# Moved in a two-layer trunk: 1/rms sums, a gate projection, filler products and stores

## The chip, the cores and the metric

The kernel runs on one core of a Trainium2 chip. The metric is the device time of one execution in microseconds (us), a median over runs. Engines: PE is TensorE, DVE is VectorE, ACT is ScalarE, POOL is GpSimd, SP is SyncE, which only issues DMAs here. PEclk is the granted clock of TensorE as a share of its full speed.

## The reference

One step of a streaming encoder trunk with two layers, on 1,024 new frames of one stream and 64 frames of another, 1,088 columns together, D_MODEL 1024, in float32. Each layer does `x += mixer(rmsnorm(x))` and then `x += sqrelu_mlp(rmsnorm(x))`; a last rmsnorm follows. Layer 0's mixer is sliding-window attention, layer 1's is a gated linear recurrence (HGRN2):

```python
def hgrn2_mix(h, s0, w_in, lb, out_norm, w_o):
    zq, zf, zi, zg = jnp.split(h @ w_in, ...)          # 8 heads of 128 each
    q = silu(zq); k = (1 - lb) * sigmoid(-zf); v = zi
    logf = jnp.log(lb + (1 - lb) * sigmoid(zf))
    o, S = hgrn_scan(q, k, v, logf, s0)                # chunks of 64 frames
    o = rmsnorm(o, out_norm) * silu(zg)
    return o.reshape(B, T, D) @ w_o, S

def sqrelu_mlp(h, w_up, w_down):                       # 1024 -> 4096 -> 1024
    return jnp.square(jax.nn.relu(h @ w_up)) @ w_down
```

## The kernel before

Activations lie with features on the partitions and the 1,088 columns along the free dimension: eight tiles of 128 features, two of them to a `pair` tile. Every product of float32 values is done as three matmuls of operands that are split in a high and a low part (high by high, high by low, low by high: lines 117, 118 and 119, in `up` lines 862 and 875). The high part is a cast on ScalarE, the low part a subtraction or a fused multiply and subtract on VectorE (line 108 for weights, 777 and 958 for activations).

The stages follow each other: attention (to about 353 us of the profiled execution), the MLP of layer 0 (to about 1134), the recurrence (to about 1740), the MLP of layer 1 (to the end). An MLP has three parts:

- `mix_rest` finishes the mixer's output projection. Output tiles d below `na` got the products of the first six input tiles already in the mixer's stage, from `mix_out`, where they serve as filler (NA = 6 tiles in attention, NB = 4 in the recurrence); `mix_rest` adds the last two input tiles for these and all eight for the others, then adds each product to x on VectorE (`mix_acc`, line 444), squares x on ScalarE and sums the squares over tiles on VectorE (`square_part`, line 157). Tiles 6 and 7 come last, in four column chunks of 272 (`CH4`). On the way it prepares the operands of `up`: b11, b12, t2, t4 and t3 for each of the four pairs of tiles.
- `up` multiplies with w_up by a Strassen-like scheme on halves of rows and columns (TH = 544 columns). The first two tiles are done plainly, by `whole(t, ps, i)`, 48 matmuls each: `whole(0, ps, 0)` needs b11 and b12, `whole(0, ps, 1)` needs b21 and b22, which `op.odd(p)` prepares. `norm(j)` multiplies the sums of squares of column half j with a matrix of ones on TensorE (line 845) and makes 1/rms from it on ScalarE and VectorE; `finish` (lines 881 to 883) applies it, squares, and stores the tile to y_mlp in HBM.
- `down` multiplies with w_down in five groups of 4, 8, 6, 8 and 6 input tiles. `hidden` loads an input tile from y_mlp (line 956, in GpSimd's DMA queue), and splits it (lines 957 and 958). x itself is parked in HBM (x_mlp) during `up` and reloaded at the start of `down`.

The recurrence makes, for each of eight heads, four projections of 72 matmuls (`proj`: f, q, v and the gate g), in three column chunks; `mix` does the scan with masked scores (its products stand at lines 601 to 696), and `tail` multiplies scores and states with v and q, normalises (lines 724 to 742) and applies the gate. The first projection goes ahead of its 1/rms: the raw product is ready in a bank of PSUM, `norm_scale` makes the sum over partitions in another (line 181) and 1/rms from it (lines 169 to 175), and VectorE multiplies (line 542). The pool `mm` has three banks there, the pool `psB` four.

The order in which each engine does its instructions isn't the written one: a planner orders them when the program is built, from estimated readiness, with the written order as priority. DMA issues are ordered in the same way in each engine's queue, and each queue is worked off in order.

Of the kernel before, what the change touches and what calls it, by code (L numbers as in the profile page):

```python
# [17 lines left out]
P = 128  # L18
# [9 lines left out]
TH = T // 2  # L28
# [5 lines left out]
EPS = 1e-5  # L34
NLEV = 5
NA = 6
NB = 4


class Trunk:  # L40
# [79 lines left out]
        return ps[:, :n], s, n  # L120


    def scaled(self, c):
        if c in self.due:
            self.due.remove(c)
            self.norm_scale(c)


    def banks(self, ctx, name, n):
# [2 lines left out]
    def bank(self):  # L132
        return self.mm.tile([P, 512], F32, name="mm", tag="mm")
# [40 lines left out]
        nc.vector.tensor_scalar(y[:, :n], y[:, :n], -0.5, 1.5, ALU.mult, ALU.add)  # L174
        nc.vector.tensor_mul(out, out, y[:, :n])

    def norm_scale(self, c):
        nc = self.nc
        s, n = self.CH[c]
        ps = self.bank()  # L180
        nc.tensor.matmul(ps[:, :n], self.ones[:], self.ss[:, s:s + n], start=True, stop=True)
        self.inv_root(self.rstd[:, s:s + n], ps[:, :n], n, D)

# [263 lines left out]
    def mix_rest(self, wa, wb, op, na):  # L447
        self.new_norm()
        ins = self.xin()

        def squares(k):
            for c in range(len(self.CH)):
                self.square_part(k, c)

        self.CH = CH64
        for d in range(6):
            if d >= na:
                w = self.weight(wa[d])
            elif d % 4 == 0:
                w = self.weight(wb[:, 2 * d:min(2 * na, 2 * d + 8), :], min(8, 2 * (na - d)))  # L460
            for c in range(3):
                if d < na:
                    self.mix_acc(w[2 * (d % 4):2 * (d % 4) + 2], ins[6:], d, c)
                else:
                    self.mix_acc(w, ins, d, c)
            squares(d)
            if d % 2:
                op.b11(d // 2)
                op.t24(d // 2)
        ws = [self.weight(wa[d]) for d in (6, 7)]  # L470
        self.CH = CH4
        for c in range(4):
            for d in (6, 7):
                self.mix_acc(ws[d - 6], ins, d, c)
        for p in range(3):
            op.b12(p)
        for p in range(3):
            op.t3(p)
        op.b11(3)
        op.b12(3)  # L480
        for d in (6, 7):
            squares(d)


    def recurrence(self):
        nc, tc, A, O = self.nc, self.tc, self.A, self.O
        with ExitStack() as ctx:
# [43 lines left out]
            def proj(piece):  # L531
                w = self.weight(A["w_in"][piece])
                z = hp.tile([P, T], F32, name="z", tag="z", bufs=3)
                ready = []
                for c in range(3):
                    if c == len(ready):
                        ready.append(self.product(w, self.xin(), c))
                    if c < 2 and c in self.due:
                        ready.append(self.product(w, self.xin(), c + 1))
                    ps, s, n = ready[c]  # L540
                    self.scaled(c)
                    nc.vector.tensor_mul(z[:, s:s + n], ps, self.rstd[:, s:s + n])
                return z

# [3 lines left out]
            def gates(h):  # L548
                r = {}
                z = proj(8 + h)  # L550
                r["f"] = f = hp.tile([P, T], F32, name="f", tag="f")
                bk = self.pair(3) if h % 2 else hp.tile([P, 2, T], F32, name="bk", tag="bk")
                r["b"], r["kk"] = b, kk = bk[:, 0, :], bk[:, 1, :]
                o_, l_ = om[:, h:h + 1], lb[:, h:h + 1]
                sig(f[:], z[:], 1.0)
                nc.vector.tensor_scalar(f[:], f[:], o_, l_, ALU.mult, ALU.add)
                t = tmp()
                nc.scalar.activation(t[:], f[:], AF.Ln)
                nc.vector.tensor_tensor_scan(b, reset[:], t[:], 0.0, ALU.mult, ALU.add)
                sig(kk, z[:], -1.0)  # L560
                nc.vector.tensor_scalar(kk, kk, o_, None, ALU.mult)

                z = proj(h)
                r["q"] = q = hp.tile([P, 9, 192], F32, name="q", tag="q", bufs=2)
                t = tmp()
                sig(t[:], z[:], 1.0)
                nc.vector.tensor_mul(q[:, :8, :P], z[:, :TP].rearrange("p (n t) -> p n t", t=P),
                                     t[:, :TP].rearrange("p (n t) -> p n t", t=P))
                nc.vector.tensor_mul(q[:, 8, :64], z[:, TP:], t[:, TP:])
                nc.vector.tensor_mul(q[:, :8, P:], q[:, :8, 1:P:2],  # L570
                                     f[:, :TP].rearrange("p (n t) -> p n t", t=P)[:, :, 1::2])
                nc.vector.tensor_mul(q[:, 8, 64:96], q[:, 8, 1:64:2], f[:, TP + 1::2])
                z = proj(16 + h)
                r["v"] = v = hp.tile([P, 9, P], F32, name="v", tag="v", bufs=2)
                for b0 in range(0, 9, 4):
                    pt = pb.tile([P, 4, P], F32, name="pv", tag="pv", bufs=1)
                    if b0 < 8:
                        for i in range(4):
                            nc.tensor.transpose(pt[:, i, :], z[:, (b0 + i) * P:(b0 + i + 1) * P], self.ident[:])
                        nc.scalar.copy(v[:, b0:b0 + 4, :], pt[:])  # L580
                    else:
                        nc.tensor.transpose(pt[:64, 0, :], z[:, TP:], self.ident[:])
                        nc.scalar.copy(v[:64, 8, :], pt[:64, 0, :])
                z = proj(24 + h)
                r["g"] = z
                t = tmp()
                sig(t[:], z[:], 1.0)
                nc.vector.scalar_tensor_tensor(z[:], z[:], on[:, 0:1], t[:], ALU.mult, ALU.mult)
                return r

            def mix(h, r):
                b, kk, q, v, g, f = r["b"], r["kk"], r["q"], r["v"], r["g"], r["f"]
                sc = sct[0]


# [18 lines left out]
                for lev in range(NLEV):  # L614
                    hh = 32 >> lev
                    ns = 32 // hh
                    d = tmp()
# [17 lines left out]
                    for i in range(17):  # L635
                        r = 64 * (i % 2)
# [3 lines left out]
                    for u in range(2):  # L640
                        r = slice(64 * u, 64 * u + 64 - hh)
# [14 lines left out]
                t = tmp()  # L656
# [4 lines left out]
                t = tmp()  # L661
# [41 lines left out]
                            e = eb[:, 2 * n:2 * n + 1]  # L703
                            nc.vector.scalar_tensor_tensor(st[:, dst, :], st[:, n, :], e, pt[:, i, :], ALU.mult, ALU.add)
                nc.sync.dma_start(O["s"][h], st[:, 9:11, :])
                return sc, v, q, st, g

            def tail(h, sc, v, q, st, g):
                p = h // 2
# [33 lines left out]

            for h in range(8):
                r = gates(h)
                tail(h, *mix(h, r))
            for _ in self.mix_out(A["hw_oa"], self.xd, NB):
                pass

# [72 lines left out]
    def up(self, ctx, layer, op, up):  # L822
        nc = self.nc
        pu = ctx.enter_context(self.tc.tile_pool(name=f"pu{layer}", bufs=4, space=PSUM))

        def acc():
            return pu.tile([P, 2, 512], F32, name="pu", tag="pu")[:, :, :TH // 2]
# [11 lines left out]
            return work[2 + j // 4][:, j % 4, :]  # L839


        def norm(j):
            out, ps = self.rstd[:, TH * j:TH * j + TH], acc()
            for c in range(2):
                nc.tensor.matmul(ps[:, c, :], self.ones[:], cols(out)[:, c, :], start=True, stop=True)
            v, y = (up.tile([P, TH], F32, name="tt", tag="tt", bufs=3)[:] for i in range(2))
            nc.vector.tensor_scalar(cols(v), ps, 1.0 / D, EPS, ALU.mult, ALU.add)
            nc.scalar.activation(out, v, AF.Ln)
            nc.scalar.activation(out, out, AF.Exp, scale=-0.5)
            nc.scalar.activation(y, out, AF.Square)  # L850
            nc.vector.tensor_mul(y, y, v)
            nc.vector.tensor_scalar(y, y, -0.5, 1.5, ALU.mult, ALU.add)
            nc.vector.tensor_mul(out, out, y)


        def whole(t, ps, i):
            w = self.parts(raw(t, i, self.wp))
            for p in range(4):
                for j in range(2):
                    for c in range(2):  # L860
                        for n, (x, y) in enumerate(((0, 0), (0, 1), (1, 0))):
                            nc.tensor.matmul(ps[j][:, c, :], w[p][x], cols(op[f"b{i + 1}{j + 1}", p][y])[:, c, :],  # L862
                                             start=i == p == n == 0, stop=i == 1 and p == 3 and n == 2)
# [14 lines left out]
        def finish(t, j, a):  # L878
            y = room("y")
            r = self.rstd[:, TH * j:TH * j + TH]  # L880
            nc.vector.scalar_tensor_tensor(cols(y), a, 0.0, cols(r), ALU.max, ALU.mult)
            nc.scalar.activation(y, y, AF.Square)
            nc.sync.dma_start(self.yk[layer][t, :, TH * j:TH * j + TH], y)

        def plus(name, ps, b):
            t = cols(room(name))
            nc.vector.tensor_tensor(t, ps, b, ALU.add)  # L887
            return t

        norm(0)  # L890
        ps = [acc(), acc()]
        whole(0, ps, 0)
        for p in range(4):
            op.odd(p)
        norm(1)
        whole(0, ps, 1)
        ps = [ps, [acc(), acc()]]
        whole(1, ps[1], 0)
# [268 lines left out]
```

## Time and profile before

| | |
|---|---|
| median of 3 runs | 2548.89 us (2548.43 to 2551.03) |
| profiled execution, its own time | 2550.03 us |
| profiled execution, span | 2548.3 us |
| mean granted clock of TensorE | 0.989 |
| busy PE, DVE, ACT, POOL | 2486.2, 1485.8, 975.6, 91.6 us |
| matmuls | 17,704 |

The profiled execution is one more execution beside the timed runs; its span is what the profile's rows add up to, and its own time has 1.7 us more. Busy time of PE is made of matmuls whose ends are modelled, at whatever clock was granted.

### The profile page before, as it was taken

The page shows a single profiled execution, that of the slowest core. Times are in us where ns is not written, and L with a number is a line of the kernel's source. Part 1 is how long each engine was busy: PE and PEld are TensorE (multiplying, and loading weights), DVE is VectorE, ACT ScalarE, POOL GpSimd, SP SyncE. Part 2 cuts the span into 40 slices and gives each one's busy share as a digit, 9 for nine tenths or more (in the row PEclk, how much of TensorE's full clock was granted, in tenths as well). Part 3 has the DMA queues.
Part 4 walks back from the last instruction along what each step waited for, and adds up shares of the span by engine and source line. Part 5 has one row for each costly group of instructions (what it writes and reads, how often), then busy time and mean ns, then how long its engine had stood idle before and what let it go on. Part 6 is the DMA issues. An engine that isn't in the chain of part 4 may idle for free.

```text
span 2548.3 us, 43611 instructions
## 1 busy us (share of the span) xinstructions
PE 2486.2 (98%) x17704; PEld 2424.9 (95%) x17704; DVE 1485.8 (58%) x2774; ACT 975.6 (38%) x2044; POOL 91.6 (4%) x209
## 2 busy tenths in 40 slices
PE   8999998999999999999999999999999999999998
PEld 7998898999999999999999999988999999999997
DVE  7555458666674243355677777876766667424335
ACT  5246545333342022134555555644533334102222
POOL 2201100000010000000000000000000001000000
PEclk9999999999999999999999999998999999999999
DMA  5312132333363133131111111123233336313311
GB/s 167 88 47 66 37 112 76 104 103 103 103 243 125 38 116 103 45 115 37 34 36 37 38 34 33 31 94 106 86 97 109 103 103 249 107 39 115 103 54 71
DMA packets 116648, 223.39 MB, mean 88 GB/s; under 512 B 29008, under 2 KB 43728, under 8 KB 112720
## 3 DMA queue, kind: packets, MB, share of 16 engines
q1 hardware_dynamic: 103360, 174.50, 21.0%
q0 software_dynamic: 13088, 46.11, 5.1%
q8 instruction: 139, 2.28, 0.4%
q14 instruction: 61, 0.50, 0.1%
HBM read 158.95 MB, written 55.05 MB: 84 GB/s over the span
## 4 chain that ended last, share of the span: by engine, by line
PE 95%; DVE 2%; DMA 1%; issue 1%; ACT 1%; SPq 0%; POOL 0%; POOLq 0%; DVEq 0%; ACTq 0%
PE pu L875 23%; PE mm L117 19%; PE mm L118 19%; PE mm L119 19%; PE pu L862 2%; PE sc L332 2%; PE po L366 2%; PE pb L637 2%; PE pb L601 1%; PE pt L360 1%; PE pb L724 1%; PE pb L696 1%; PE pb L726 1%; PE pb L739 0%; PE pb L668 0%
## 5 line engine op out<-in xcount | busy, mean ns | idle before, releaser
L117 PE MATMUL mm<-xh,whi 128*128 128x384 f32 (+4 forms) x2208 | 731.2, 332 | 16.0 <-ACT whi L107 11.9
L118 PE MATMUL mm<-xl,whi 128*128 128x384 f32 (+4 forms) x2208 | 727.4, 330 | 0.0
L119 PE MATMUL mm<-xh,wlo 128*128 128x384 f32 (+4 forms) x2208 | 725.7, 329 | 0.0
L107 ACT CAST whi<-raw 128x512 fp32r<-128x512 f32 (+1 forms) x351 | 197.0, 596 | 651.4 <-PE mm L118 540.2
L117 PEld LDWEIGHTS mm<-xh,whi 128*128 128x128 f32 x2208 | 417.5, 189 | 22.8 <-ACT whi L107 12.9
L444 DVE TENSOR_TENSOR pair<-pair,mm 128x362 f32<-128x362 f32 (+4 forms) x322 | 167.9, 525 | 438.7 <-PE mm L119 432.1
L118 PEld LDWEIGHTS mm<-xl,whi 128*128 128x128 f32 x2208 | 417.5, 189 | 4.4 <-issue 3.3
L119 PEld LDWEIGHTS mm<-xh,wlo 128*128 128x128 f32 x2208 | 417.3, 189 | 2.9 <-issue 0.9
L875 PE MATMUL pu<-xh,wlo 128*128 128x272 f32 x960 | 277.0, 289 | 0.0
L875 PE MATMUL pu<-xl,whi 128*128 128x272 f32 x960 | 275.6, 287 | 0.0
L875 PE MATMUL pu<-xh,whi 128*128 128x272 f32 x960 | 275.5, 287 | 0.0
L108 DVE TENSOR_TENSOR wlo<-raw,whi 128x512 fp32r<-128x512 f32 (+1 forms) x351 | 222.2, 660 | 15.3 <-ACT whi L107 14.8
L117 PE MATMUL mm<-eh,whi 128*128 128x362 f32 (+1 forms) x624 | 205.7, 330 | 7.2 <-DVE pair L887 7.2
L875 PE MATMUL pu<-eh,wlo 128*128 128x272 f32 x720 | 208.0, 289 | 0.0
L875 PE MATMUL pu<-eh,whi 128*128 128x272 f32 x720 | 207.6, 288 | 0.1
L887 DVE TENSOR_TENSOR pair<-pu,pair 128x544 f32<-128x544 f32 x150 | 108.5, 724 | 169.0 <-PE pu L875 160.9
L875 PE MATMUL pu<-el,whi 128*128 128x272 f32 x720 | 207.0, 287 | 0.0
L118 PE MATMUL mm<-el,whi 128*128 128x362 f32 (+1 forms) x624 | 205.3, 329 | 0.0
L119 PE MATMUL mm<-eh,wlo 128*128 128x362 f32 (+1 forms) x624 | 204.3, 327 | 0.3 <-DVE wlo L108 0.3
L875 PEld LDWEIGHTS pu<-xh,whi 128*128 128x128 f32 x960 | 180.9, 188 | 0.0
L875 PEld LDWEIGHTS pu<-xl,whi 128*128 128x128 f32 x960 | 180.5, 188 | 0.0
L875 PEld LDWEIGHTS pu<-xh,wlo 128*128 128x128 f32 x960 | 180.2, 188 | 0.0
(277 smaller groups left out, 3948.6 us busy)
## 6 DMA issues: line engine op xcount, KB each, us to landing
y_mlp<-pair SPq DMA_DIRECT2D x128, 272.0 KB, 2.1
raw<-in_w_up SPq DMA_DIRECT2D x128, 256.0 KB, 2.7
raw<-in_w_down SPq DMA_DIRECT2D x112, 256.0 KB, 3.0
el<-y_mlp POOLq DMA_DIRECT2D x32, 544.0 KB, 7.4
xl<-y_mlp POOLq DMA_DIRECT2D x32, 544.0 KB, 7.9
raw<-in_w_in SPq DMA_DIRECT2D x64, 256.0 KB, 2.7
x_mlp<-pair SPq DMA_DIRECT2D x8, 1088.0 KB, 4.8
pair<-x_mlp SPq DMA_DIRECT2D x8, 1088.0 KB, 8.8
```

The costliest lines, as they stand in the source:

```text
L107: nc.scalar.copy(hi, raw)
L108: nc.vector.tensor_sub(lo, raw, hi.bitcast(F32))
L117: nc.tensor.matmul(ps[:, :n], wh, ih[:, s:s + n], start=i == 0, stop=False)
L118: nc.tensor.matmul(ps[:, :n], wh, il[:, s:s + n], start=False, stop=False)
L119: nc.tensor.matmul(ps[:, :n], wl, ih[:, s:s + n], start=False, stop=i == last)
L332: nc.tensor.matmul(ps[u][:, i, :kn], st, kd[g][r, k0:k0 + kn], start=True, stop=True)
L366: nc.tensor.matmul(out, ptts[u][:, kt, :], v, start=start, stop=stop)
L444: self.nc.vector.tensor_add(self.x(d)[:, s:s + n], self.x(d)[:, s:s + n], ps)
L637: nc.tensor.matmul(psa[r:r + 64 - hh, i // 2, :].rearrange("p (s t) -> p s t", t=hh), d[:, i * 64:i * 64 + 64 - hh], dv[:, i * ns:(i + 1) ...
L862: nc.tensor.matmul(ps[j][:, c, :], w[p][x], cols(op[f"b{i + 1}{j + 1}", p][y])[:, c, :], start=i == p == n == 0, stop=i == 1 and p == 3 an ...
L875: nc.tensor.matmul(ps[:, c, :], a, cols(b)[:, c, :], start=not more and p == i == 0, stop=p == 3 and i == 2, skip_group_check=True)
L887: nc.vector.tensor_tensor(t, ps, b, ALU.add)
```

## The change

Six edits: `mix_out` of the recurrence does six output tiles instead of four (NB); the 1/rms sums of the recurrence's first projection go to a bank of `psB`; a head's gate projection stands behind `mix`; at the end of `mix_rest` the squares of tiles 6 and 7 of the first two column chunks come ahead of the operand preparations, the rest behind them, and t3 last; the sums of `up` for both halves stand behind `whole(0, ps, 0)` and `op.odd`, in two accumulators taken first (`self.half = None` makes the next weights take a new tile); and `finish` stores through GpSimd's queue.

```diff
-NB = 4
+NB = 6
-    def scaled(self, c):
+    def scaled(self, c, bank=None):
         if c in self.due:
             self.due.remove(c)
-            self.norm_scale(c)
+            self.norm_scale(c, bank([P, 512]) if bank else self.bank())
...
-    def norm_scale(self, c):
+    def norm_scale(self, c, ps):
         nc = self.nc
         s, n = self.CH[c]
-        ps = self.bank()
...
             for d in (6, 7):
                 self.mix_acc(ws[d - 6], ins, d, c)
-        for p in range(3):
-            op.b12(p)
+        for j in range(2):
+            for d in (6, 7):
+                for c in (2 * j, 2 * j + 1):
+                    self.square_part(d, c)
+            if j == 0:
+                for p in range(3):
+                    op.b12(p)
+                op.b11(3)
+                op.b12(3)
         for p in range(3):
             op.t3(p)
-        op.b11(3)
-        op.b12(3)
-        for d in (6, 7):
-            squares(d)
...
-                    self.scaled(c)
+                    self.scaled(c, bank)
                     nc.vector.tensor_mul(z[:, s:s + n], ps, self.rstd[:, s:s + n])
...
+                return r
+
+            def gate(h):
                 z = proj(24 + h)
-                r["g"] = z
                 t = tmp()
                 sig(t[:], z[:], 1.0)
                 nc.vector.scalar_tensor_tensor(z[:], z[:], on[:, 0:1], t[:], ALU.mult, ALU.mult)
-                return r
+                return z
...
                 r = gates(h)
-                tail(h, *mix(h, r))
+                m = mix(h, r)
+                tail(h, *m, gate(h))
...
-        def norm(j):
-            out, ps = self.rstd[:, TH * j:TH * j + TH], acc()
+        def norm(j, ps):
+            out = self.rstd[:, TH * j:TH * j + TH]
...
-            nc.sync.dma_start(self.yk[layer][t, :, TH * j:TH * j + TH], y)
+            nc.gpsimd.dma_start(self.yk[layer][t, :, TH * j:TH * j + TH], y)
...
-        norm(0)
+        pn = [acc(), acc()]
         ps = [acc(), acc()]
         whole(0, ps, 0)
+        self.half = None
         for p in range(4):
             op.odd(p)
-        norm(1)
+        for j in range(2):
+            norm(j, pn[j])
         whole(0, ps, 1)
```

## Rows read from the trace of the kernel before

**Rows 1.** The page: busy time of each engine with its share of the span and its instructions, and the chain of work that ended last by engine.

```profile
PE 2486.2 (98%) x17704; PEld 2424.9 (95%) x17704; DVE 1485.8 (58%) x2774; ACT 975.6 (38%) x2044; POOL 91.6 (4%) x209
...
PE 95%; DVE 2%; DMA 1%; issue 1%; ACT 1%; SPq 0%; POOL 0%; POOLq 0%; DVEq 0%; ACTq 0%
```

**Rows 2.** The waits of PE: the waiting line, what it waited for, and us in total, how often, the longest.

```profile
PE pu L845 <- DVE ss L157: 7.9, 1, 7.9
PE mm L117 <- DVE pair L887: 7.2, 2, 5.0
PE pb L668 <- DVE q L664: 5.4, 1, 5.4
...
PE mm L117 <- DVE n L170: 2.4, 2, 1.3
PE mm L181 <- DVE n L170: 1.7, 1, 1.7
PE pu L845 <- DVE pair L444: 1.6, 1, 1.6
```

**Rows 3.** Windows: from and to, the width, the busy time of PE, PEld, DVE, ACT and POOL with the number of instructions, PE's granted clock, the DMA share, GB/s.

```profile
353.00:397.40 44.40, 44.18 (x300) 43.96 (x300) 39.78 (x75) 27.24 (x52) 0.00 (x0) 0.95 0.40 137
397.40:415.10 17.70, 9.84 (x58) 9.39 (x59) 14.57 (x26) 11.23 (x21) 0.00 (x0) 0.81 0.36 123
1153.09:1156.50 3.41, 3.38 (x11) 3.38 (x12) 2.80 (x6) 0.91 (x2) 0.00 (x0) 0.50 0.00 2
1640.00:1709.00 69.00, 69.00 (x592) 66.00 (x591) 57.19 (x126) 40.37 (x93) 0.00 (x0) 1.00 0.24 85
1709.80:1739.70 29.90, 17.98 (x90) 13.46 (x87) 14.27 (x37) 11.74 (x45) 0.00 (x0) 0.67 0.18 60
1739.70:1801.40 61.70, 61.65 (x408) 61.43 (x408) 46.09 (x86) 31.92 (x59) 0.00 (x0) 0.97 0.26 90
```

**Rows 4.** The chain that ended last, in order of time, where layer 0's `mix_rest` meets `up`: start, duration, engine and line, instructions.

```profile
405.26 1.24 PE pu L845 x2
...
414.16 0.92 PE pu L845 x4
415.08 17.99 PE pu L862 x144
```

**Rows 5.** The same chain in layer 1, `whole(0, ps, 0)`.

```profile
1804.11 6.02 PE pu L862 x48
```

**Rows 6.** VectorE's timeline where layer 0's `mix_rest` meets `up`: start, duration, engine, line, operation, shapes, how many.

```profile
399.12 2.86 DVE L777 SCALAR_TENSOR_TENSOR xl<-pair,gains,xh 128x544 fp32r<-128x544 f32 x4
...
410.82 0.43 DVE L157 TENSOR_TENSOR ss<-ss,n 128x272 f32<-128x272 f32 x1
```

**Rows 7.** The chain at the start of the recurrence.

```profile
1143.11 0.66 PE mm L181 x2
...
1148.70 0.63 ACT whi L107
...
1153.12 0.69 PE mm L117
```

**Rows 8.** The chain in `mix` of head 6 and of head 7: the same two groups of products in each.

```profile
1645.42 1.08 PE pb L668 x16
...
1656.51 2.20 PE pb L696 x18
...
1715.29 1.95 PE pb L668 x16
...
1720.20 3.65 PE pb L696 x18
```

**Rows 9.** GpSimd's timeline at the turn from up to down of layer 0: start, duration, line, operation, how many; in brackets the idle time before and what ended it.

```profile
732.01 1.77 POOL L956 DMA_DIRECT2D el<-y_mlp  x3 [409.76 <-PE pu L875]
734.00 0.53 POOL L956 DMA_DIRECT2D el<-y_mlp  x1 [0.22 <-PE pu L875]
```

**Rows 10.** The timeline of SyncE's DMA queue at the same turn.

```profile
732.65 0.32 SPq L982 DMA_DIRECT2D pair<-x_mlp  x1
743.05 1.87 SPq L883 DMA_DIRECT2D y_mlp<-pair  x2
...
751.57 0.32 SPq L883 DMA_DIRECT2D y_mlp<-pair  x1
...
754.68 0.32 SPq L883 DMA_DIRECT2D y_mlp<-pair  x1
```

**Rows 11.** VectorE's timeline at the same turn: the last splits of the four `el` tiles, the read of the last accumulator of `up`, and the first adds of `down` that use a reloaded x.

```profile
743.61 2.48 DVE L958 TENSOR_TENSOR el<-el,eh 128x1088 fp32r<-128x1088 f32 x2
...
750.30 0.72 DVE L887 TENSOR_TENSOR pair<-pu,pair 128x544 f32<-128x544 f32 x1
...
776.03 2.74 DVE L444 TENSOR_TENSOR pair<-pair,mm 128x364 f32<-128x364 f32 x6 [5.46 <-DMA raw<-in_w_down]
```

**Rows 12.** The DMA issues by kind: out and in, queue, operation, how many, KB each, median us from issue to landing.

```profile
y_mlp<-pair SPq DMA_DIRECT2D x128, 272.0 KB, 2.1
...
xl<-y_mlp POOLq DMA_DIRECT2D x32, 544.0 KB, 7.9
raw<-in_w_in SPq DMA_DIRECT2D x64, 256.0 KB, 2.7
...
raw<-in_w_qkv POOLq DMA_DIRECT2D x24, 256.0 KB, 3.5
```

More of the change, by code (lines that the diff above doesn't have):

```diff
@@ L588, in gates @@
                 nc.vector.scalar_tensor_tensor(z[:], z[:], on[:, 0:1], t[:], ALU.mult, ALU.mult)
-                return r
+                return z
             def mix(h, r):
-                b, kk, q, v, g, f = r["b"], r["kk"], r["q"], r["v"], r["g"], r["f"]
+                b, kk, q, v, f = r["b"], r["kk"], r["q"], r["v"], r["f"]
                 sc = sct[0]
@@ L705, in mix @@
                 nc.sync.dma_start(O["s"][h], st[:, 9:11, :])
-                return sc, v, q, st, g
+                return sc, v, q, st
             def tail(h, sc, v, q, st, g):
```

## The prediction

> **What bounds the kernel now.** I read the page first: TensorE (PE) is busy 98% of the span and is 95% of the chain that ended last, the other engines 58% and less [rows 1]. So only two things can move the time: PE's idle time and PE's busy time at half clock. The diff adds and drops no matrix product. Next come the waits of PE: those that the diff can touch are 7.9 us for the 1/rms sum of layer 0's MLP, 1.6 us for that of layer 1, 7.2 us in two waits at the turns from up to down, 5.4 us in head 7 of the recurrence and 4.1 us in three waits at its start [rows 2]. Last come the windows, where the reader is to see that from 1709.8 to 1739.7 PE is busy 17.98 us of 29.90 at a granted clock of 0.67, while the 69 us before have no idle time and a clock of 1.00 [rows 3]. All sums are made against the profiled execution, 2550.03 us, which lies 1.14 us above the median of the runs (2548.89).
>
> **A. The sums of layer 0's MLP go behind half a plain tile.** PE's last product of the stage before ends at 397.40, the first sum runs at 405.26, the 48 matmuls of `whole(0, ps, 0)` follow with the other sums between them, and `whole(0, ps, 1)` starts at 415.08 [rows 3, 4]: 17.68 us. The same 48 matmuls with nothing between them took 6.02 us in layer 1 [rows 5]; eight sum matmuls at 0.23 us (0.92 for four [rows 4]) are 1.85. Floor 7.9, most that can be won 9.8. What is late next is VectorE: it is busy 14.57 of those 17.70 us [rows 3], with operand splits from 399.12 and the last add of squares ending at 411.25 [rows 6]. In the new order `whole(0, ps, 0)` waits for `b11(3)` and `b12(3)`, not for squares, but `whole(0, ps, 1)` wants eight splits of `odd()` at 0.71 us (2.86 for four [rows 6]) right behind it, and the t3 steps and the norm's own operations compete for the same engine. I take 1.5 us of stall: **−8.3**. Bounds: −4 (eight splits, 5.7 us, all uncovered) and −9.8. The weight pair that `self.half = None` no longer shares costs one more turn of a ring and no instruction: 0.
>
> **B. The recurrence's first sums go to the other pool.** From the first sum at 1143.11 to the first matmul of the second projection at 1153.12 are 10.0 us [rows 7]. In them the third product waits 1.3 us for a bank [rows 2], because the sum took one of three; it runs from 1143.77 + 1.26 to 1148.70, where the casts of the second projection's weights, which wait for its end, begin [rows 7]: 3.7 us. With the sum elsewhere it can follow at once, and the casts come forward with it: three sums at 0.66 [rows 7] and 3.7 are 5.7, so −4.3. The second projection ran its first 3.41 us at clock 0.50 [rows 3], which is 1.7 us of lost work. Ceiling −6.0; nothing in the row says that one gap less would leave a half-clock stretch, so I take **−5.5**, bounds −4 and −6.
>
> **C. The end of the recurrence gets filler.** With NB from 4 to 6, two more output tiles over six heads are done behind the heads: 2 tiles × 3 column chunks × 6 heads × 3 products = 108 matmuls, which are taken from layer 1's `mix_rest` (it has 408, layer 0's has 300 [rows 3]). They are worth 61.65 − 44.18 = 17.5 us [rows 3]. With the gate's projection behind `mix`, head 7 has 72 more matmuls, at the same 0.162 us 11.7 us, that need nothing of the scores: 29.2 us of filler in all. What it can fill: 29.90 − 17.98 = 11.9 us idle. What the clock can give back: 17.98 us at 0.67 would be 12.0 at full clock, 5.9 us; the next window's 61.65 at 0.97 adds up to 1.9, so 7.8 at most; two groups alone (L668 takes 1.08 in head 6 and 1.95 in head 7, L696 2.20 and 3.65 [rows 8]) prove 2.3. I take 6.5. Ceiling 18.4. The filler's adds (six more at 0.46 us [rows 11]) and splits of weights stand in VectorE's queue beside the tail's chain; it is busy 14.27 of 29.90 us there [rows 3], so there is room. But PE has no idle time at all in the 69 us ahead of the gaps [rows 3], with filler of the same kind in them: whether the new filler is kept for the gaps is the planner's choice. I leave 3.4 us of gaps: **−15**, bounds −3 (the filler is used up early; only the gate's projection helps the 5.4 us wait [rows 2]) and −18.4. Earlier heads run like the 69 us of head 6, without idle time, so the later gate is worth 0 there; should it open gaps, its own 11.7 us stand ready to fill them.
>
> **D. The seam of layer 1.** It loses those 17.5 us of PE work under which VectorE caught up: VectorE is busy 46.09 of 61.70 us there, in layer 0 39.78 of 44.40 [rows 3]. So it comes to look like layer 0's new seam, where I leave a 1.5 us stall; now it has 1.6 [rows 2]: **0**, bounds −1.6 and +3.
>
> **E. Stores of activations to GpSimd's queue.** 128 stores of 272 KB, 64 a layer [rows 12]. GpSimd issues one in 0.53 us [rows 9] and does nothing else in up, and PE waits for no weight in up that SyncE's queue would now bring earlier [rows 2], so nothing is won or lost there. Loads of 256 KB land in 2.7 us from SyncE's queue and in 3.5 from GpSimd's [rows 12]: a store may land 0.8 us later. The x_mlp reload waits for the last store: issued 754.68, and the add that uses the reload runs at 776.03 [rows 10, 11]. PE would feel it only at the 15th product, which wants the bank of the seventh: 751.16 + 14 products of 12 matmuls at 0.167 (2.0 us) = 779.2; the add takes 0.46, so the cover is 2.6 us. Behind the reload in SyncE's queue stand loads of w_down, which would come late with it. The queue that a store is moved past holds the loads of `hidden`; they are the first rival. The bank wait at the turn (7.2 us in two [rows 2]) hangs on L887 behind the splits L958 in VectorE's queue [rows 11], which stay. **0**, bounds −5 and +4.
> A rule of the Trainium skill speaks against this part: "SBUF — State Buffer", section "SBUF: two separate sides", says that GpSimd can't write the descriptors of a DMA from its queue while VectorE runs an operation in a two-port mode, and advises ScalarE's or SyncE's queue. By it stores would land late in stretches full of such operations; the 0.53 us issues next to busy VectorE [rows 9, 11] show no such wait, and by the rows the price is 0.
>
> Sum: −8.3 − 5.5 − 15 + 0 + 0 = −28.8; 2550.03 − 28.8 = 2521.2 profiled, 2520 as a median.
>
> **The rivals.**
> *Loads behind the last stores (the other side).* GpSimd's queue is in order. The first down product starts at 751.16 (0.14 behind L887's end [rows 11]) and needs four `el` loads, issued from 732.01 to 734.00, the last split 12.1 us after its issue (746.09) [rows 9, 11]; it is wanted 9 matmuls (1.5 us) into the product. Stand the four behind the store that went out at 754.68 [rows 10], they end at 754.68 + 0.53 + 1.99 + 12.09 = 769.3, and PE is 16.6 us late; behind that of 751.57, 13.5 us; behind that of 743.05, 5.0. In two layers 27 to 33 us, and some 2 us of half clock after each: +31 to +37, so 2551 to 2557. It decides from the last two stores on; behind earlier ones the gain stays. Against it: in SyncE's queue a reload was issued at 732.65 ahead of earlier-written stores at 743.05, so the queue follows readiness and not the text. Chance 0.08.
> *The filler is used up early.* C gives −3: −16.8, 2532. For it: PE is already full for 69 us ahead of the gaps [rows 3]. Against it: 29 us more stand against 18. Chance 0.16.
> *VectorE becomes the bound at both seams.* A −4 and D +3: −21.5, 2527. For it: VectorE's share there; against it: t3 can wait. Chance 0.13.
> *Everything fills.* −9.8 − 6 − 18.4 − 1.6 is −35.8, and up to −5 at the turns: 2508 to 2513. Chance 0.12.
> *Late stores.* Store descriptors wait for VectorE, the last store lands as late as the slow loads do, so the reload is 5.8 us late (7.9 less 2.1, medians [rows 12]): 3.2 us of stall in layer 0, with some half clock +5: 2525, inside the main case's range. With two other mishaps it ends slower; I keep 0.02 for that. The Trainium skill's rule above would be its cause.
> *The plan hardly changes.* The planner sorts PE's instructions anyway, and an edit of written order may not move them: 2549. Chance 0.06; the waits that the diff takes away are waits for data and banks, not for order.
>
> **How the numbers follow.** Main case (2513 to 2528) 0.43. A measurement here can tell about 0.2%, 5.1 us. Faster: 0.43 + 0.16 + 0.13 + 0.12 = 0.84; same 0.06; slower 0.08 + 0.02 = 0.10. The range takes in the main case, the used-up filler, VectorE's bound and the low end: 2508 to 2538.
>
> **What would show it.** A: the sums stand behind 48 matmuls, PE's gap at 397 is under 2 us and VectorE's splits end the rest. B: no wait of PE for n L170 between the first products. C: the window from head 7's scores to the mix has PE above 85% and clock above 0.9. D: `mix_rest` of layer 1 has 300 matmuls and some 44 us. E: GpSimd issues 128 stores of median 2.1 to 3.5 us and PE's wait at the turns stays near 7 us. Wrong if el loads are issued after 743, if PE's wait for VectorE at the layer-1 seam passes 5 us, or if the tail's window still has 8 us idle.

## The result and the profile after

The changed kernel takes 2516.57 us (median of 4 runs, 2515.82 to 2516.95) against 2548.72 for the kernel before in the same set: a ratio of 0.9872, 95% interval 0.9854 to 0.9889, 32 us faster. The profiled execution took 2516.2 us with a span of 2514.2, 34.1 less than the span before.

Both spans cut at the same five points show where that lies. First the kernel before, then the changed one; the cuts are the end of PE's last product ahead of layer 0's `up`, the end of that `up`, of that `down`, of the recurrence with layer 1's `mix_rest`, and of layer 1's `up`. Columns as in [rows 3].

```profile
0.00:397.40 397.40, 381.56 (x2452) 354.38 (x2452) 227.61 (x577) 190.88 (x627) 56.76 (x144) 0.99 0.28 84
397.40:748.87 351.47, 343.61 (x2720) 342.94 (x2720) 229.87 (x349) 133.11 (x222) 6.87 (x13) 0.99 0.35 113
748.87:1133.83 384.96, 382.41 (x2304) 381.79 (x2304) 160.47 (x265) 90.15 (x148) 10.01 (x19) 1.00 0.29 101
1133.83:1801.35 667.52, 650.76 (x5199) 620.47 (x5198) 476.85 (x969) 348.99 (x704) 1.06 (x1) 0.98 0.15 49
1801.35:2145.19 343.84, 342.15 (x2720) 341.43 (x2720) 222.03 (x337) 128.81 (x214) 6.85 (x13) 1.00 0.35 117
2145.19:2548.30 403.11, 385.74 (x2311) 383.91 (x2310) 169.00 (x281) 83.66 (x133) 10.02 (x19) 0.98 0.28 96
```

```profile
0.00:395.26 395.26, 379.33 (x2452) 352.36 (x2452) 227.60 (x577) 190.83 (x627) 56.91 (x144) 1.00 0.28 84
395.26:739.59 344.33, 342.29 (x2720) 341.56 (x2720) 229.28 (x349) 133.01 (x222) 39.96 (x74) 1.00 0.35 116
739.59:1124.13 384.54, 382.13 (x2304) 381.86 (x2304) 160.28 (x265) 90.26 (x148) 11.59 (x22) 1.00 0.29 102
1124.13:1770.17 646.04, 640.63 (x5198) 615.95 (x5198) 472.38 (x966) 342.41 (x695) 1.06 (x1) 0.99 0.16 51
1770.17:2114.87 344.70, 342.69 (x2720) 341.42 (x2720) 229.52 (x349) 133.91 (x225) 39.98 (x74) 1.00 0.34 115
2114.87:2514.20 399.33, 384.37 (x2311) 382.53 (x2310) 166.40 (x279) 83.91 (x133) 11.59 (x22) 0.99 0.28 97
```

From top to bottom the stretches differ by −2.1, −7.1, −0.4, −21.5, +0.9 and −3.8 us. PE's matmuls are the same in number (up to a record), so a difference is idle time (width less busy) or busy time, which grows where the clock is at half. The first, attention and layer 0's `mix_rest`, is no gain of the change: its idle time is the same (15.8 and 15.9 us), the difference is clock, and that varies from one execution to the next. In the profiles of the experiments below it ended between 394.1 and 395.3 in eleven and at 399.3 in one.

The waits of PE after, to be read beside [rows 2]; lines have moved a little with the change (444 is now 443, 738 is 742, 862 is 867, 883 is 888, 887 is 892, 982 is 989). The 7.9 us for the sums, the 5.4 us in head 7 and the three at the start of the recurrence are gone. New at the seams are 2.0 us, ended by the last add of `mix_rest` (L443), in layer 0 and 1.4 us, ended by the cast of an operand, in layer 1. The wait at the turn is 2.4 us instead of 2.3 in layer 0 and 2.8 us instead of 5.0 in layer 1.

```profile
PE pb L743 <- ACT hon L742: 3.5, 5, 1.5
PE mm L117 <- DVE pair L892: 2.8, 1, 2.8
PE mm L117 <- ACT pair L887: 2.4, 1, 2.4
PE pu L867 <- DVE pair L443: 2.0, 1, 2.0
...
PE pu L867 <- ACT xh L781: 1.4, 1, 1.4
```

The windows after that answer to [rows 3]: layer 0's seam, the start of the recurrence (three sums and the third product), the tail, the stretch at half clock at its end, and layer 1's `mix_rest`.

```profile
395.30:413.05 17.75, 15.75 (x119) 15.46 (x120) 15.96 (x29) 11.92 (x22) 0.00 (x0) 1.00 0.36 123
1133.40:1138.60 5.20, 5.20 (x32) 4.51 (x31) 3.08 (x6) 2.78 (x6) 0.00 (x0) 1.00 0.01 3
...
1697.00:1725.60 28.60, 24.17 (x151) 22.35 (x150) 11.57 (x33) 9.87 (x42) 0.00 (x0) 0.98 0.16 51
1724.21:1731.04 6.83, 5.82 (x19) 5.64 (x20) 2.09 (x4) 1.96 (x5) 0.00 (x0) 0.50 0.22 77
1725.60:1770.20 44.60, 44.57 (x300) 44.35 (x300) 38.64 (x73) 25.30 (x47) 0.00 (x0) 0.94 0.33 114
```

The seam has 2.0 us idle instead of 7.9 and full clock instead of 0.81; the tail has 4.4 us idle instead of 11.9; `mix_rest` is 300 matmuls long. The tail's clock of 0.98 against 0.67 flatters the change, because most of its stretch at half clock, 6.83 us from 1724.21, lies behind the window. The kernel before had 23.9 us at half clock there, in two stretches:

```profile
1712.87:1723.11 10.24, 7.03 (x40) 6.82 (x41) 4.52 (x9) 2.17 (x5) 0.00 (x0) 0.50 0.33 97
1729.94:1743.59 13.65, 9.75 (x28) 6.78 (x29) 5.01 (x15) 6.64 (x26) 0.00 (x0) 0.50 0.12 38
```

### The profile page after: what moved, and what is told of

It is laid out like the page before. It is cut to its first block, busy times and chain, and to the rows that moved or that the text cites. A ratio compares the mean times of both kernels' runs of the same rounds, so it can differ in the third digit from the quotient of the medians.

```text
span 2514.2 us, 43600 instructions
## 1 busy us (share of the span) xinstructions
PE 2471.4 (98%) x17704; PEld 2415.7 (96%) x17704; DVE 1485.5 (59%) x2781; ACT 974.3 (39%) x2045; POOL 161.1 (6%) x337
## 4 chain that ended last, share of the span: by engine, by line
PE 96%; DVE 1%; DMA 1%; ACT 1%; issue 1%; POOL 0%; SPq 0%; POOLq 0%; ACTq 0%; DVEq 0%
PE pu L880 24%; PE mm L117 20%; PE mm L118 19%; PE mm L119 19%; PE sc L331 2%; PE po L365 2%; PE pb L641 2%; PE pu L867 1%; PE pb L605 1%; PE pt L359 1%; PE pb L728 1%; PE pb L700 1%; PE pb L730 1%; PE pb L743 0%; PE pb L672 0%
## 5 line engine op out<-in xcount | busy, mean ns | idle before, releaser
L107 ACT CAST whi<-raw 128x512 fp32r<-128x512 f32 x352 | 197.5, 596 | 655.7 <-PE mm L118 547.8
L443 DVE TENSOR_TENSOR pair<-pair,mm 128x362 f32<-128x362 f32 (+4 forms) x328 | 170.2, 525 | 433.3 <-PE mm L119 431.6
L108 DVE TENSOR_TENSOR wlo<-raw,whi 128x512 fp32r<-128x512 f32 x352 | 222.5, 658 | 19.1 <-ACT whi L107 18.5
```

The source lines that it names most:

```text
L107: nc.scalar.copy(hi, raw)
L108: nc.vector.tensor_sub(lo, raw, hi.bitcast(F32))
L443: self.nc.vector.tensor_add(self.x(d)[:, s:s + n], self.x(d)[:, s:s + n], ps)
```

## The experiments

Each is the changed kernel with one edit, or with several where the text says so; e9 is the changed kernel itself. Ratios are to the kernel before, run in the same set; the changed kernel itself had 0.9872 in its first set and 0.9878 in the last one (e9). Spans are of one profiled execution each, 2514.2 and 2513.9 for the changed kernel; differences of spans are to their mean.

**The fillers at the recurrence's end, one at a time and both.** NB alone (e1):

```diff
-NB = 6
+NB = 4
```

> The changed kernel (2516.6 us) with NB back at 4, all else kept. Theory (both fillers are needed at the end of the recurrence): the gate's 11.7 us still cover head 7's wait, but 17.5 us of filler are gone from the tail and its gaps and its half clock return: 8 to 12 us slower, 2525 to 2529, with layer 1's mix_rest back at 408 matmuls. Rival 1 (the gate's projection alone closes the gaps): 2516 to 2519. Rival 2 (NB alone does it): some 15 us slower, 2532.

The gate's projection alone (e2):

```diff
-                return r
-
-            def gate(h):
                 z = proj(24 + h)
...
-                tail(h, *m, gate(h))
+                tail(h, *m, r["g"])
```

> The changed kernel with the gate's projection back ahead of mix. Theory (both fillers are needed): head 7's wait for its q (5.4 us in the kernel before) comes back in part and the tail runs out of filler earlier: 5 to 9 us slower, 2522 to 2526. Rival (NB's 17.5 us of filler are enough): 2516 to 2519.

Both edits together (e5):

> The changed kernel with both fillers of the recurrence's end undone: NB at 4 and the gate ahead of mix. Theory after the first runs (either filler alone covers most of the same 18.4 us, so undoing one costs 2 to 4 us and undoing both costs the whole of it): ratio to the kernel before 0.993 to 0.995, some 14 to 18 us above the changed kernel. Rival (each part is worth only what its own undoing cost, 2 to 4 us, and the rest of the gain at the recurrence's end has another cause): 0.9895 to 0.991.

Measured: e1 2520.11 us, 0.9884 (0.9868 to 0.9900), span 2517.5; e2 2521.07 us, 0.9883 (0.9867 to 0.9900), span 2518.5; e5 2529.64 us, 0.9926 (0.9908 to 0.9944), span 2525.9. So one filler undone costs 1 to 4 us (by ratio it can't be told from the changed kernel, by span it is 3.4 and 4.4), both 12 to 14 us by ratio and 11.8 by span. My theory that each filler is needed fell with e1 and e2: with either one, head 7's wait of 5.4 us is gone. The two are substitutes. The joint cost of 12 to 14 us lies a little below the 14 to 18 that I had then expected, and far above twice the single one. With both undone the tail is nearly that of the kernel before, with 11.7 us idle instead of 11.9 (29.90, 17.98 and 0.67 in [rows 3]), and head 7's wait is back to the tenth:

```profile
1693.20:1722.60 29.40, 17.70 (x89) 13.02 (x86) 14.38 (x37) 11.82 (x45) 0.00 (x0) 0.65 0.18 61
```

```profile
PE pb L670 <- DVE q L666: 5.4, 1, 5.4
```

With NB alone undone, the last 35 us of the recurrence have 4.5 us of idle time where the changed kernel's tail has 4.4. Clock is part of the difference: 10.02 us of busy time at half clock against 5.82, which is 2.1 us lost. The second turn, too, has 3.41 us at half clock in this execution, layer 1's seam gives 1.8 us back, and the rest isn't broken down:

```profile
1675.00:1710.00 35.00, 30.52 (x212) 26.02 (x210) 20.70 (x49) 16.68 (x50) 0.00 (x0) 0.89 0.25 82
...
1702.20:1715.85 13.65, 10.02 (x29) 7.04 (x30) 4.94 (x15) 6.38 (x24) 0.00 (x0) 0.50 0.12 38
```

So what is left at the end is not a lack of filler in sum: in the changed kernel the filler is spent before the last two of the chain's three blocks. e11 takes that up.

**The order at the seams from `mix_rest` to `up`, all of it (e3) and the end of `mix_rest` alone (e10).** In e3

```diff
...
-        pn = [acc(), acc()]
+        norm(0)
         ps = [acc(), acc()]
         whole(0, ps, 0)
-        self.half = None
         for p in range(4):
             op.odd(p)
-        for j in range(2):
-            norm(j, pn[j])
+        norm(1)
         whole(0, ps, 1)
```

with the end of `mix_rest` as before too; in e10 that alone:

> The changed kernel with the end of mix_rest and the start of up as before (sums of the first half ahead of the first plain tile). Theory (the parts interact: with NB at 6 layer 1's seam has no cover either, so it too gets the wait that layer 0 had): PE waits about 8 us for the sums in both layers, 14 to 17 us slower, 2531 to 2534. Rival (the parts add up, only layer 0 loses its 7 us): 2523 to 2525.

> The changed kernel with only the end of mix_rest as before (t3 ahead of b11(3) and b12(3), all squares of tiles 6 and 7 last); the sums stay behind the first half tile. Theory (the place of the sums is what counts, but VectorE is the bound at the seam and its order decides the rest): the first half tile waits for its last splits behind t3, 2 to 5 us in each layer, so 4 to 10 us slower than the changed kernel. Rival (the planner's order by readiness makes the written order of squares and t3 indifferent): within 1.5 us of the changed kernel.

Measured: e3 2531.35 us, 0.9924 (0.9909 to 0.9940), 12 to 13 us slower; e10, in which only the end of `mix_rest` is as before, 2516.67 us, 0.9883 (0.9866 to 0.9901), span 2513.2: no difference that can be told. Cut at the same points as above, `up` with its seam takes 351.1 us in layer 0 and 350.1 in layer 1 in e3, against 344.3 and 344.7 in the changed kernel and 344.3 and 344.7 in e10. PE's waits in e3:

```profile
PE pu L847 <- DVE ss L157: 13.4, 2, 7.9
```

That is two waits, 7.9 and 5.5 us, where the kernel before had one of 7.9 and one of 1.6 [rows 2]. So the parts interact, as the theory says: with NB at 6 the work that covered layer 1's sums has gone to the recurrence, and only the new order of `up` keeps its seam short. The size is a little below the 14 to 17 us I gave, since the second wait is 5.5 and not 8. And e10 shows that the rewritten end of `mix_rest` has no part in it: its theory fell, the rival held. The waits at the seams (2.0 and 1.4 us) are the same to the tenth in both orders.

**The bank of the first 1/rms sums (e6).**

```diff
-                    self.scaled(c, bank)
+                    self.scaled(c)
```

> The changed kernel with the recurrence's first 1/rms sums back in a bank of mm. Theory (the bank sets the start): the three waits of 1.1 to 1.7 us and the half-clock stretch return, 4 to 6 us slower, ratio to the kernel before 0.9888 to 0.9896. Rival (the norm's chain of operations sets the start, not the bank): within 1.5 us of the changed kernel, 0.9866 to 0.9878.

Measured: 2528.49 us, 0.9910 (0.9895 to 0.9924), span 2521.2. The ratio is 8 to 10 us above the changed kernel's, with single runs from 2524 to 2530, and the span 7.2. The three waits are back to the tenth ([rows 2] has the same two lines), and with them the stretch of 3.41 us at half clock:

```profile
PE mm L117 <- DVE n L170: 2.4, 2, 1.3
...
PE mm L180 <- DVE n L170: 1.7, 1, 1.7
```

Waits and stretch are 5.8 us, as expected; the rest of the span's 7.2 is clock (10.24 us at half clock in the tail where the changed kernel had 6.83, and 3.41 at the second turn), and whether that belongs to the edit stays open. The bank sets the start, the norm's chain doesn't.

**The queue of the stores, and what it does at the turns (e4, e7).** In e4 the stores are back in SyncE's queue:

```diff
-            nc.gpsimd.dma_start(self.yk[layer][t, :, TH * j:TH * j + TH], y)
+            nc.sync.dma_start(self.yk[layer][t, :, TH * j:TH * j + TH], y)
```

> The changed kernel with the stores of y_mlp back in SyncE's queue. Theory (the stores have no part in the gain): 2515.5 to 2518. Rival (the 3.8 us that the turn from up to down of layer 1 and its half-clock stretch are shorter by come from the stores): 2519 to 2521.

Measured: 2523.70 us, 0.9899 (0.9882 to 0.9915), span 2521.8: 5 to 7 us slower by ratio, with intervals that overlap a little, and 7.7 by span. The trace has the cost at the turns, where PE waits 9.7 us instead of 5.2 and runs 3.41 us at half clock behind each wait, where the changed kernel has none:

```profile
PE mm L117 <- DVE pair L892: 9.7, 2, 5.0
```

My theory fell, and the cost is above the rival's too. The loads of `hidden` are issued at the same time in both kernels, so the queue's order isn't it. What differs is when the first reload of x_mlp (1088 KB) goes out beside them, and how long the first `el` load (544 KB) then takes. Timelines of GpSimd, SyncE's queue, ScalarE and VectorE at layer 0's turn, the stores in SyncE's queue:

```profile
722.72 1.77 POOL L963 DMA_DIRECT2D el<-y_mlp  x3 [401.55 <-DMA y_mlp<-pair]
...
722.88 0.32 SPq L989 DMA_DIRECT2D pair<-x_mlp  x1
...
729.32 1.10 ACT L964 CAST eh<-el 128x1088 fp32r<-128x1088 f32 x1 [6.16 <-DMA el<-y_mlp]
...
743.40 0.72 DVE L892 TENSOR_TENSOR pair<-pu,pair 128x544 f32<-128x544 f32 x1
```

and the changed kernel:

```profile
722.73 1.07 POOL L963 DMA_DIRECT2D el<-y_mlp  x2 [1.14 <-PE pu L880]
...
723.48 0.33 SPq L989 DMA_DIRECT2D pair<-x_mlp  x1
...
726.98 1.10 ACT L964 CAST eh<-el 128x1088 fp32r<-128x1088 f32 x1 [3.81 <-DMA el<-y_mlp]
...
741.14 0.72 DVE L892 TENSOR_TENSOR pair<-pu,pair 128x544 f32<-128x544 f32 x1
```

The reload waits for the y tiles of the step before to be stored. From GpSimd's queue the store ahead of it goes out 0.3 us later than from SyncE's (721.04 against 720.76), and a store lands in 2.4 us instead of 2.1 [rows 12],

```profile
y_mlp<-pair POOLq DMA_DIRECT2D x128, 272.0 KB, 2.4
```

so the reload goes out 0.75 us behind the first `el` load instead of 0.16. In the first case the load is cast 4.25 us after its issue, in the second 6.6. VectorE's splits come 2.3 us later, and so does the read of `up`'s last accumulator behind them. Before, layer 0 had a reload 0.64 us behind (732.65 against 732.01, [rows 9, 10]) and a cast after 4.0; layer 1 had 0.46 us and 7.5, and its turn cost 5.0 us and not 2.3:

```profile
2128.26 2.27 POOL L956 DMA_DIRECT2D el<-y_mlp  x4 [993.31 <-PE pu L875]
...
2128.72 0.32 SPq L982 DMA_DIRECT2D pair<-x_mlp  x1
...
2135.73 1.10 ACT L957 CAST eh<-el 128x1088 fp32r<-128x1088 f32 x1 [4.82 <-DMA el<-y_mlp]
```

To part the reload from the stores, in e7 the stores are in SyncE's queue as in e4 and the reload is moved:

```diff
-                    nc.sync.dma_start(self.xp[p][:], self.xk[layer][:, 2 * p:2 * p + 2, :])
+                    (nc.sync if p else nc.gpsimd).dma_start(self.xp[p][:], self.xk[layer][:, 2 * p:2 * p + 2, :])
```

> Stores of y_mlp back in SyncE's queue as in e4_sp, but the first reload of x_mlp stands in GpSimd's queue behind the first two el loads. Theory (in e4_sp the reload was issued 0.16 to 0.20 us behind the first el load and shared the DMA engines with it, so the load landed in 6.6 to 6.9 us instead of 4.3, and the splits on VectorE and the read of up's last accumulator came 2.3 us later): the first el cast starts 4.0 to 4.5 us after its load's issue, PE waits under 3 us at both turns, ratio 0.9865 to 0.988, as the changed kernel. Rival (it is the stores in SyncE's queue themselves, whatever the reload does): 0.989 to 0.9905, as e4_sp.

Measured: 2515.10 us, 0.9865 (0.9851 to 0.9880), span 2512.9, at the level of the changed kernel and with an interval wholly below e4's; PE's waits at the turns are 4.9 us in two. The reload goes out 1.2 us behind the first load, whose cast starts after 4.0 us (725.54 against 721.56), in layer 1 after 4.6:

```profile
721.56 1.12 POOL L963 DMA_DIRECT2D el<-y_mlp  x2 [401.28 <-DMA y_mlp<-pair]
722.75 0.53 POOL L989 DMA_DIRECT2D pair<-x_mlp  x1
...
725.54 1.10 ACT L964 CAST eh<-el 128x1088 fp32r<-128x1088 f32 x1 [3.54 <-DMA el<-y_mlp]
```

So it was the reload beside the load and not the stores' queue as such. The Trainium skill says in "DMA: Bandwidth & Descriptors", section "Issuing engines are not separate DMA queues", that DMAs of different issuing engines end on the same 16 DMA engines and interleave there; the landing of the load, 4.0 to 4.6 us or 6.6 to 7.5 by the reload's distance, agrees.

**What is left at the turns (e8).** VectorE's splits for the next ten tiles, which nobody needs yet, are ordered behind the last read of an accumulator:

```diff
...
-            nc.vector.tensor_sub(hl[:], y, hh[:].bitcast(F32))
+            with tc.issue_after(self.read) if GROUPS[0] <= t < 14 else ExitStack():
+                nc.vector.tensor_sub(hl[:], y, hh[:].bitcast(F32))
```

(`self.read` is the last addition of `plus`.)

> The changed kernel, with the splits of the second group of down's tiles (VectorE, the xl subtractions) ordered behind the last read of up's accumulators. Theory (what is left of the wait at the turns, 2.4 and 2.8 us, is VectorE busy with these early splits when the last accumulator comes free): both waits fall to 1 us or so, 3 to 5 us faster than the changed kernel, ratio 0.985 to 0.986. Rival (another thing ends the wait, a cast or a load): no change, 0.9868 to 0.9878.

Measured: 2513.02 us, 0.9852 (0.9837 to 0.9867), span 2510.6. The interval overlaps that of the changed kernel, but the two waits, 5.2 us there, are 1.8 us in sum, and the span is 3.5 us shorter:

```profile
PE mm L117 <- DVE pair L892: 1.8, 2, 0.9
```

**What is left at the recurrence's end (e11, e12).** In the changed kernel's last block each normalisation on ScalarE (L742) waits for the transpose of the one before on PE, though it reads another part of the bank:

```profile
1722.65 0.36 ACT L742 ACTIVATE hon<-pb,hrs 128x128 f32<-128x128 f32 x1
1723.43 0.37 ACT L742 ACTIVATE hon<-pb,hrs 128x128 f32<-128x128 f32 x1 [0.42 <-PE pb L743]
1724.22 0.36 ACT L742 ACTIVATE hon<-pb,hrs 64x128 f32<-64x128 f32 x1 [0.42 <-PE pb L743]
```

In e11, which has the edit of e8 too, the loop is written as two, and the three normalisations come first; e12 adds the edits of e7:

```diff
                         nc.scalar.activation(on_[r_, i, :], po[r_, i, :], AF.Copy, scale=rs[r_, i:i + 1])
+                    for i in range(3):
+                        n = b0 + i
+                        cn = P if n < 8 else 64
+                        r_ = slice(0, cn)
                         nc.tensor.transpose(pt[:, i, :cn], on_[r_, i, :], self.ident[r_, :cn])
```

> The changed kernel once more, unedited, for the comparison within this set: ratio to the kernel before 0.986 to 0.9885, PE waits of 2.2 to 2.8 us at both turns and of 4 to 5 us in sum at the end of the recurrence.

> The changed kernel with the edit of e8_turn and with the tail's three normalisations of a block written ahead of its three transposes. Theory (in the last 7 us of the recurrence each normalisation on ScalarE waits for the transpose before it, about 0.8 us a step, and no filler is left): the last gaps shrink by 1 to 2 us and the half-clock stretch with them, 1 to 4 us faster than e8_turn, 4 to 8 us faster than the changed kernel. Rival (the chain waits for the norm's small operations, not for the transposes): as e8_turn, 3 to 5 us faster than the changed kernel.

> The edits of e11_turn_tail2 and of e7_sp_late together: stores of y_mlp in SyncE's queue, the first x_mlp reload behind two el loads in GpSimd's. Theory (with the read of the last accumulator ahead of the early splits, the queue of the stores no longer matters, as long as the first el load isn't late): within 1.5 us of e11_turn_tail2. Rival (the stores in SyncE's queue free GpSimd's queue for the loads of the turn, which is why e7_sp_late stood a little below the changed kernel): 1.5 to 4 us faster than e11_turn_tail2.

Measured in one set: the changed kernel 2515.86 us, 0.9878 (0.9862 to 0.9894); e11 2502.76 us, 0.9827 (0.9811 to 0.9843), the fastest of all, 13 us below the changed kernel and some 45 below the kernel before; e12 2504.54 us, 0.9831 (0.9816 to 0.9846), no different from it. The changed kernel's turns wait 5.1 us in sum here. e11 gained more than either expectation: its tail has a single gap of 0.6 us where the changed kernel had 4.4 us idle and a stretch of 6.83 us at half clock,

```profile
1697.00:1717.10 20.10, 19.52 (x123) 18.38 (x121) 9.04 (x24) 7.56 (x26) 0.00 (x0) 1.00 0.16 52
```

and in its trace 12 matmuls of filler still follow the chain's last transpose: the shorter chain ends while there is filler left. The trace also shows where the filler had gone. In the changed kernel 18 and 19 matmuls of it stand between the three transposes (L743) of the tail's first block, which are 3.4 to 3.7 us apart, and none behind them:

```profile
1711.10 0.27 PE L743 MATMUL pb<-ident,hon 128*128 128x128 f32 x1
...
1714.79 0.27 PE L743 MATMUL pb<-ident,hon 128*128 128x128 f32 x1
...
1718.15 0.27 PE L743 MATMUL pb<-ident,hon 128*128 128x128 f32 x1
```

In e11 the three transposes of a block stand together, and 38 and 47 matmuls of filler stand between the blocks:

```profile
1704.82 0.49 PE L747 MATMUL pb<-ident,hon 128*128 128x128 f32 x3
```

So the edit does two things, it takes away the waits from step to step and moves the filler to where the chain waits, and no run parts the two. Nor was it run without e8's edit; by the spans of e8 and the changed kernel, some 3.5 us of the 13 are e8's. In e12 the stores' queue makes no difference that can be told once the early splits are out of the way, as its theory says; its rival fell.

## Why the prediction was right, point by point

The time of 2516.57 us lies 3.4 us below the 2520 that were predicted, inside the main case's 2513 to 2528. By its terms:

- **A, −8.3: −7.1 measured** (the second stretch). Right in the main: the sums stand behind the 48 matmuls of the first half tile, at full clock, and e3 without this order is 6.8 us longer there. The stall is 2.0 us where I left 1.5 (and gave under 2 as the sign), but it is not the one I priced. `whole(0, ps, 1)` never waits for its eight splits; PE waits ahead of `whole(0, ps, 0)`, and by the chain what ends the wait is the last add of `mix_rest`, behind operand work in VectorE's queue. That the two sizes agree is luck. That the rewritten end of `mix_rest` would matter for it was my reading of the diff; e10 shows that it doesn't. The chain after, where `mix_rest` of layer 0 meets `up`:

```profile
396.72 0.44 DVE pair L443
397.16 0.14 issue
397.30 6.52 PE pu L867 x50
403.82 0.46 PE pu L850 x2
```

- **B, −5.5: −6.0 measured.** From the first sum to the start of the 49th matmul of the products behind it are 15.97 us before, 9.93 after and 16.01 in e6. The half-clock stretch went entirely, which I had left open.
- **C, −15: −15.5 measured** (−21.5 for the recurrence and `mix_rest`, less B). The sum was right, the picture behind it not. Idle time fell by 7.0 us where I took 8.5, and busy time by 8.4 where I took 6.5 and called 7.8 the most. That ceiling was read wrong: a mean clock of 0.67 over a window with idle time hides that 16.8 us of busy time (7.03 and 9.75) ran at half clock, 8.4 us to win, of which the 5.82 us that still run so leave 5.5; the other 2.9 us of busy time the rows don't put down to anything. So it is in part luck that the sum comes out. The window has PE at 84.5%, just under the 85% that I gave as the sign. I took the fillers as adding up to 29.2 us against 18.4 and worried that the first would be used up early. It was used up before the last two of the chain's blocks, and yet either filler alone buys all but 1 to 4 us; what remained in the tail (4.4 us idle) went with the chain's own written order (e11), which I had not looked at.
- **D, 0: +0.9 measured.** Layer 1's seam waits 1.4 us, as layer 0's waits 2.0. e3 shows that this zero is a gain of its own: with the old order the seam waits 5.5 us.
- **E, 0: −0.4 and −3.8 measured**, the one term that was mis-sized. In layer 1 the wait is 2.2 us shorter, and the rest is a stretch of 3.41 us at half clock that is gone; e1, e3 and e6 have such a stretch at that turn with the short form of the wait, so this rest isn't shown to be the change's. I wrote that the bank wait at the turn hangs on L887 behind the splits in VectorE's queue, "which stay". The first half is right (e8); the second is the step that failed. The splits don't stay: they move with the landing of the `el` loads, and that moves with the x_mlp reload, which waits for the stores whose queue the change alters. I had the reload's delay in hand (0.8 us, landing in GpSimd's queue) and counted it only as a risk; the cover that I set against it is 2.7 us by my own figures and not 2.6, which changes nothing. Against the changed kernel with the old queue the part is worth 5 to 7 us (e4), because there both turns have the slow form; in the profile of before only one had.
- The remaining −2.1 us is the clock in attention, and no part of the change; it is about what the profiled difference (33.8 us) has over that of the medians (32.2).

The first rival stayed off: all four `el` loads went out by 724.72, ahead of the stores of 733.62 to 745.75. The late stores came, by 0.3 us and not by 5.8, and their effect had the other sign. The Trainium skill's rule ("SBUF — State Buffer", section "SBUF: two separate sides") would have stores from GpSimd's queue starve while VectorE runs an operation in a two-port mode. VectorE is busy 229 of 344 us in `up`, and the stores land in 2.4 us against 2.1. No row tells in which mode VectorE's operations ran, so the runs don't test the rule, and nothing tells what those 0.3 us are made of.

## What to carry to other kernels

Two fillers for the same gaps don't add up: price them against the idle time together, and undo them one by one and both before crediting either. When a DMA's queue is changed, look at what waits for it and at what that then collides with; here a reload that left 0.6 us later was worth several times as much. And before more filler is fetched for a serial tail, count the chain's steps that wait for nothing but a written order.

## What the runs showed of the hardware

A load of 544 KB whose neighbour is a 1088 KB reload was cast 4.0 to 4.6 us after its issue where the reload was issued 0.64 us or more behind it, and 6.6 to 7.5 us where it was issued 0.16 to 0.46 us behind it: of the 28 turns before, after and in e1 to e12, 25 are of the first kind and 3 of the second (layer 1's before, both of e4). The distance alone is not the measure, since the 7.5 us belong to 0.46 and not to 0.16. How the engines share the two transfers within that time was not tried. And a stretch of half clock is no fixed price of a stage: attention, which is the same in all kernels, had a stretch of 3.41 us near 286 us in some executions (before, e3, e8) and not in others, and one execution of e12 had 10.24 us at 236 us, some 5 us of its span. Nor does the length of the wait decide it: at layer 1's turn a wait of 2.8 us had no such stretch behind it in the changed kernel and one of 2.7 us had 3.41 us in e6.
